# Weight tiles, row fetches and two of four weight sums of a Strassen-type product: DVE additions replaced by adding transfers from GpSimd

## The chip, the core and the metric

One of the eight cores of a Trainium2 chip runs the whole layer as one program. The metric is the device time of one execution in microseconds (us), as the median of several runs. Engines are called as in the profile: PE is TensorE's matrix multiply, PEld its weight load, DVE is VectorE, ACT is ScalarE, POOL is GpSimd and SP is SyncE. SP and POOL mostly issue transfers here: each has a queue that is worked through in order, and an issue that waits holds up everything behind it on that queue.

## The reference, cut to what matters

```python
h = rms_norm(x, norm_in_g[layer])
proj = jnp.einsum('bsd,de->bse', h, w_in[layer])              # 512 x 2048 times 2048 x 19456
(qa, ka, va, za, qb, kb, vb, zb, qm, zm, gates) = jnp.split(proj, split_points, axis=-1)
...                                                            # three attention branches, each * silu(gate path)
g_a, g_b, g_m = jnp.split(jax.nn.sigmoid(gates), N_BRANCH, axis=-1)
merged = (g_a * (ya @ w_proj_a) + g_b * (yb @ w_proj_b) + g_m * (ym @ w_proj_m))
x = x + jnp.einsum('bsd,de->bse', merged, w_out[layer])
return rms_norm(x, norm_final_g)
```

Everything is float32. 512 tokens, width 2048. Most of the work is the product of the normed input with `w_in`; the last is the product of `merged` with `w_out`.

## The kernel before

A float32 operand is split into a rounded part (`whi`, by ACT) and the remainder (`wlo`, by DVE: the tile less the rounded part), and a product is three matmuls: high times high, high times low, low times high. A weight tile is 128 partitions by 1024 columns, 0.5 MB.

**Pairs.** 65 pairs of 128-column units of `w_in` are computed by the class `Pair`: a block product with seven multiplications in place of eight (Winograd's form). The four weight quarters of a pair are called a11 and a12 (first unit, lower and upper half of the depth), a21 and a22 (second unit). Four sums of quarters are needed beside the quarters themselves: s = a21 + a22 (line 436), s + a11 (line 441), a21 + a11 (line 448) and the first s + a11 form plus a12 (line 454: s, already holding a21 + a22 + a11, plus a12). All four are DVE additions on 128x1024 tiles in SBUF. The kernel's signs and forms are arranged so that only additions are needed.

A pair runs in seven steps of 24 matmuls. The weights of the steps are, in order: p1 = a11, p5 = a21 + a22, p6 = that + a11, p2 = a12, q7 = a21 + a11, q3 = p6's tile + a12, p4 = a22. The function `parts_1024` splits each one: ACT writes `whi` (line 387), DVE writes `wlo` (line 388). There are three `whi` and three `wlo` buffers, so the split for a step starts when PE has finished the step three before. Step 3's result x is copied to SBUF by ACT (`hb`, line 456) after the third multiplication (p6), because the fifth (q7) adds on into the same PSUM bank; line 467 reads that bank again after the fifth, before the seventh (p4) adds into it.

**Where the weights come from.** SP issues the four quarter loads of a pair when the pair begins, which is in the last step of the pair before (`self.follower.begin()`). The tiles come from the pool `raw` with 18 buffers. From the forms' preparation on, 12 of these hold the input's forms T1, T2 and T3 until the last pair, so six are left for weight tiles, and a load waits until the buffer's last reader is done.

**Stages.** Memory keys and values; memory-attention queries; a branch with 8 heads (16 pairs); a dilated branch (20 pairs); then the gates: 8 rounds i of 3 pairs each. After each gate pair, DVE multiplies both results with projected rows that POOL fetched from DRAM (`pj`) and adds them up. After the third pair of round i, `merged_forms(i)` makes the forms of the merged rows i and 8+i (lines 920 to 923) and POOL stores them to DRAM (`waiting`, `waiting3`).

**The last product.** `multiply` runs the same seven-step scheme on `w_out`, twice (28 pieces each), with the sums of `w_out` quarters made by DVE. The forms stored in `waiting` are fetched back one row at a time by POOL (`fetch_then`, line 936, into slots of 512 columns or half tiles of 256), a few jobs ahead (`ahead_by`), and split by ACT and DVE into the tiles that held the input's forms (`left`, `right`, `third_form`). Which piece a job stands beside is given by the dictionary `beside`. POOL also fetches rows of x (`res`) and stores and fetches finished rows (`rows_done`).

The Tile framework writes each engine's instructions in one fixed order at build time, by its own estimates, and adds semaphore waits. At run time each engine keeps to that order.

Of the kernel before, what the change touches and what calls it, by code (L numbers as in the profile page):

```python
# [41 lines left out]
def trunk_layer(ctx: ExitStack, tc: tile.TileContext, x, xT, mem, memT, gains, gfin, w_in, w_mem, w_pa, w_pb,  # L42
# [16 lines left out]
    def wide_tile(name, dt=F32):  # L59

        return sb.tile([P, 1024], dt, name=name, tag="raw", bufs=RAWS)
# [314 lines left out]
    def quarter(u, half):  # L376
        raw = wide_tile("raw")
        nc.sync.dma_start(raw, w_in[u][:, half * 1024:(half + 1) * 1024])
        return raw

    def half_tile(name):
        return sb.tile([P, 256], F32, name=name, tag="halft", bufs=4)
# [25 lines left out]
    class Pair:  # L408
# [22 lines left out]
        def steps(self):  # L431
            u1, u2 = self.units
            a11, a21, a22, a12 = quarter(u1, 0), quarter(u2, 0), quarter(u2, 1), quarter(u1, 1)
            s = wide_tile("raw")
            p1 = parts_1024(a11)
            nc.vector.tensor_tensor(s, a21, a22, op=OP.add)  # L436
            yield 0
            p5 = parts_1024(s)
            x = acc_bank()[:, :256]
# [7 lines left out]
            seven(y, p5, "T1", start=True)  # L447
            nc.vector.tensor_tensor(a21, a21, a11, op=OP.add)
            d = half_tile("hd")
# [3 lines left out]
            seven(x, p6, "T2")  # L453
            nc.vector.tensor_tensor(s, s, a12, op=OP.add)  # L454
            b = half_tile("hb")
# [7 lines left out]
            yield 4  # L463
            q3 = parts_1024(s)
            seven(x, q7, "T3")
            g2 = self.g2 = slot("g2")
# [446 lines left out]
    waiting = dram.tile([NK, P, 512], F32, name="waiting")  # L913
    waiting3 = dram.tile([8, P, 256], F32, name="waiting3")

    def merged_forms(k):
        g0, g1 = merged[k], merged[8 + k]
        b11, b12, b21, b22 = g0[:, :256], g0[:, 256:], g1[:, :256], g1[:, 256:]
        u, v = slot("u"), half_tile("v")
        nc.vector.tensor_tensor(u[:, :256], b11, b12, op=OP.subtract)  # L920
        nc.vector.tensor_tensor(v, b22, b12, op=OP.subtract)
        nc.vector.scalar_tensor_tensor(u[:, 256:], u[:, :256], -1.0, b22, op0=OP.mult, op1=OP.subtract)
        nc.vector.scalar_tensor_tensor(b12, u[:, 256:], -1.0, b21, op0=OP.mult, op1=OP.subtract)
        for at, t in ((waiting[k], g0), (waiting[8 + k], g1), (waiting3[k], v)):
            nc.gpsimd.dma_start(at, t)
        two = split(u)
        M["T1"][k] = [p[:, :256] for p in two]
        M["T2"][k] = [p[:, 256:] for p in two]

    def fetch_then(src, shape, use):  # L930

        got = []

        def fetch():
            t = slot("mg") if shape == 512 else half_tile("mg")
            nc.gpsimd.dma_start(t, src)
            got.append(t)

        return fetch, lambda: use(got[0])

    def ahead_by(n, jobs):

        fetches, uses = zip(*jobs)

        def piece(i):
            def run():
                for f in fetches[0 if i == 0 else i + n:i + n + 1]:
                    f()
                uses[i]()
            return run  # L950

        return [piece(i) for i in range(len(jobs))]

    def left(k, form):
        c = slice(0, 256) if form == "B11" else slice(256, 512)
        return fetch_then(waiting[k][:, c], 256, lambda t: split(t, M[form][k]))

    def right(k):
        return fetch_then(waiting[8 + k], 512, lambda t: split(t, kept[8 + k]))

    def third_form(k):
        def use(t):
            if k % 2 == 0:
                M["store"] = wide_tile("T3", F32R)
            h = M["store"][:, k % 2 * 512:(k % 2 + 1) * 512]
            M["T3"][k] = split(t, (h[:, :256], h[:, 256:]))
        return fetch_then(waiting3[k], 256, use)

# [121 lines left out]
    for i in range(8):  # L1090
        pair = (i, 8 + i)
        for n, b in enumerate((0, 1, 2)):
            prs = [fetched(projected[b * NK + dt], "pj") for dt in pair]
            done = gates[i][n]
            if i == 7 and n == 2:
                done.run(2)
                later.extend(ahead_by(2, [left(k, "B11") for k in range(7)]))
                done.run(4)
                prepare(0)
# [12 lines left out]
    beside = {}  # L1112
    for at, job in zip([4 + k for k in range(8)] + [12 + k // 2 for k in range(8)] + [16 + k for k in range(8)],
                       ahead_by(3, [right(k) for k in range(8)] + [third_form(k) for k in range(8)]
                                + [left(k, "T4") for k in range(8)])):
        beside.setdefault(at, []).append(job)
    for cp in range(2):
# [17 lines left out]
        if cp:  # L1135
# [4 lines left out]
            for t in (2, 3, 0, 1):  # L1140
                for c in range(2):
                    rs[t, c] = fetched(rows_done[t, c], "res")
            for at, c in ((46, 0), (47, 1), (48, 3)):
                beside[at] = [lambda c=c: [gained(t, c) for t in (2, 3)]]
            for at, c in ((49, 0), (50, 1), (51, 2)):
                beside[at] = [lambda c=c: [gained(t, c) for t in (0, 1)]]
        multiply(zs, n + 12, "B21", True, True)
# [98 lines left out]
```

## Time and profile before

| What | Value |
|---|---|
| Median of 3 runs | 2002.5 us (2000.59 to 2006.08) |
| The profiled execution | 2006.96 us, its span 2005.2 us |
| PE busy | 1962.0 us, 98% of the span |
| DVE busy | 1530.9 us, 76% |
| ACT busy | 1020.6 us, 51% |
| Mean granted TensorE clock | 0.995 |
| Moved by DMA | 284.82 MB, mean 142 GB/s |

The span starts with the first instruction. Busy time of PE says that a matmul was in the pipeline. The granted clock is 1.00 for 2.4 GHz and falls towards 0.5 for stretches at 1.2 GHz.

### The profile page before, as it was taken

The numbers are of one execution on the slowest core, as the hardware profiler recorded it, in microseconds if no ns is written. First come the engines' busy times: TensorE is split into PE (matmuls) and PEld (weight loads), VectorE is DVE, ScalarE is ACT, GpSimd is POOL, SyncE is SP. The second block draws the span as 40 slices with busy tenths as digits, with TensorE's granted clock in tenths as the row PEclk, the third lists the DMA queues.
The fourth block names the chain that finished last, engine by engine and source line by source line (L and its number), as shares of the span: only waits on it lengthen the run. The fifth ranks groups of instructions, "written<-read, shape, count | busy, mean of one in ns | idle before, by whom it ended". The sixth has DMA issues, their size and how long they took to land.

```text
span 2005.2 us, 34840 instructions
## 1 busy us (share of the span) xinstructions
PE 1962.0 (98%) x14225; PEld 1848.9 (92%) x14225; DVE 1530.9 (76%) x1954; ACT 1020.6 (51%) x1573; POOL 135.3 (7%) x257
## 2 busy tenths in 40 slices
PE   8999999999999999999999999999999999998898
PEld 6889999789999999889999999989999999997676
DVE  5976777259989898258888889747888788777877
ACT  7654565245556665235445464644544444444535
POOL 0000010100000000010000000012000000012210
PEclk9999999999999999999999999999999999999999
DMA  9564434432332334423332322255344443347744
GB/s 365 187 224 154 131 127 148 136 106 98 98 107 94 101 106 153 142 95 96 111 99 91 113 88 98 90 176 188 112 143 148 150 140 128 128 143 275 267 179 147
DMA packets 90017, 284.82 MB, mean 142 GB/s; under 512 B 16672, under 2 KB 17696, under 8 KB 89856
## 3 DMA queue, kind: packets, MB, share of 16 engines
q1 hardware_dynamic: 71904, 225.02, 33.5%
q0 software_dynamic: 17808, 57.56, 8.4%
q8 instruction: 111, 1.82, 0.4%
q14 instruction: 50, 0.41, 0.1%
q10 hardware_dynamic: 144, 0.02, 0.0%
HBM read 251.05 MB, written 31.49 MB: 141 GB/s over the span
## 4 chain that ended last, share of the span: by engine, by line
PE 81%; DVE 6%; DMA 6%; issue 4%; ACT 1%; POOL 1%; ACTq 0%; DVEq 0%; SPq 0%; POOLq 0%
PE acc L397 18%; PE acc L398 18%; PE acc L399 18%; PE acc L112 5%; PE acc L110 5%; PE acc L111 5%; DMA raw<-in_w_in 2%; DVE wlo L388 2%; DMA mg<-waiting 2%; DMA rows_done<-res 1%; PE acc L1043 1%; PE acc L1044 1%; PE acc L1042 1%; ACT whi L387 1%; PE att L162 1%
## 5 line engine op out<-in xcount | busy, mean ns | idle before, releaser
L387 ACT ACTIVATE whi<-raw 128x1024 fp32r<-128x1024 f32 x507 | 537.2, 1060 | 604.0 <-PE acc L398 366.8
L388 DVE TENSOR_TENSOR wlo<-raw,whi 128x1024 fp32r<-128x1024 f32 x507 | 618.0, 1220 | 175.5 <-ACT whi L387 164.7
L397 PE MATMUL acc<-kept,whi 128*128 128x256 f32 x2080 | 588.6, 283 | 11.7 <-DVE g L467 10.9
L398 PE MATMUL acc<-kept,whi 128*128 128x256 f32 x2080 | 585.2, 281 | 0.0
L399 PE MATMUL acc<-kept,wlo 128*128 128x256 f32 x2080 | 584.9, 281 | 0.0
L397 PE MATMUL acc<-T,whi 128*128 128x256 f32 x1560 | 441.7, 283 | 0.5 <-ACT ha L443 0.5
L398 PE MATMUL acc<-T,whi 128*128 128x256 f32 x1560 | 441.0, 283 | 0.0
L399 PE MATMUL acc<-T,wlo 128*128 128x256 f32 x1560 | 441.0, 283 | 0.0
L397 PEld LDWEIGHTS acc<-kept,whi 128*128 128x128 f32 x2080 | 392.8, 189 | 13.7 <-issue 12.8
L398 PEld LDWEIGHTS acc<-kept,whi 128*128 128x128 f32 x2080 | 393.2, 189 | 0.4
L399 PEld LDWEIGHTS acc<-kept,wlo 128*128 128x128 f32 x2080 | 393.2, 189 | 0.0
L397 PEld LDWEIGHTS acc<-T,whi 128*128 128x128 f32 x1560 | 297.9, 191 | 1.0 <-ACT ha L443 0.7
L398 PEld LDWEIGHTS acc<-T,whi 128*128 128x128 f32 x1560 | 298.3, 191 | 0.3
L399 PEld LDWEIGHTS acc<-T,wlo 128*128 128x128 f32 x1560 | 298.2, 191 | 0.0
L91 DVE TENSOR_TENSOR wlo<-raw,whi 128x1024 fp32r<-128x1024 f32 x78 | 94.9, 1223 | 140.7 <-ACT whi L90 140.7
L90 ACT ACTIVATE whi<-raw 128x1024 fp32r<-128x1024 f32 x78 | 82.2, 1059 | 158.9 <-PE acc L111 100.8
L110 PE MATMUL acc<-shi,whi 128*128 128x512 f32 x320 | 126.6, 396 | 0.5 <-ACT pr L145 0.5
L111 PE MATMUL acc<-slo,whi 128*128 128x512 f32 x320 | 126.5, 395 | 0.0
L112 PE MATMUL acc<-shi,wlo 128*128 128x512 f32 x320 | 126.4, 395 | 0.0
L436 DVE TENSOR_TENSOR raw<-raw 128x1024 f32<-128x1024 f32 x65 | 79.5, 1223 | 25.9 <-DMA raw<-in_w_in 24.2
L441 DVE TENSOR_TENSOR raw<-raw 128x1024 f32<-128x1024 f32 x65 | 79.3, 1220 | 0.9
L454 DVE TENSOR_TENSOR raw<-raw 128x1024 f32<-128x1024 f32 x65 | 79.3, 1220 | 0.9
(269 smaller groups left out, 2609.7 us busy)
## 6 DMA issues: line engine op xcount, KB each, us to landing
raw<-in_w_in SPq DMA_DIRECT2D x266, 512.0 KB, 3.7
raw<-in_w_out SPq DMA_DIRECT2D x48, 512.0 KB, 6.5
raw<-in_w_mem SPq DMA_DIRECT2D x32, 512.0 KB, 5.1
projected<-pr POOLq DMA_DIRECT2D x48, 256.0 KB, 2.5
pj<-projected POOLq DMA_DIRECT2D x48, 256.0 KB, 5.4
raw<-in_w_pm SPq DMA_DIRECT2D x16, 512.0 KB, 3.8
raw<-in_w_pa SPq DMA_DIRECT2D x16, 512.0 KB, 4.1
xraw<-in_xT SPq DMA_DIRECT2D x16, 256.0 KB, 6.9
```

The lines of the kernel that those rows point to most:

```text
L90: nc.scalar.activation(hi, raw, AF.Copy)
L91: nc.vector.tensor_tensor(lo, raw, hi.bitcast(F32), op=OP.subtract)
L110: nc.tensor.matmul(ps, whi, hi[i], start=i == 0, stop=False)
L111: nc.tensor.matmul(ps, whi, lo[i], start=False, stop=False)
L112: nc.tensor.matmul(ps, wlo, hi[i], start=False, stop=i == n - 1)
L387: nc.scalar.activation(hi, raw, AF.Copy)
L388: nc.vector.tensor_tensor(lo, raw, hi.bitcast(F32), op=OP.subtract)
L397: nc.tensor.matmul(ps, hi[:, sl], f[0], start=start and k == 0, stop=False, skip_group_check=True)
L398: nc.tensor.matmul(ps, hi[:, sl], f[1], start=False, stop=False, skip_group_check=True)
L399: nc.tensor.matmul(ps, lo[:, sl], f[0], start=False, stop=stop and k == 7, skip_group_check=True)
L436: nc.vector.tensor_tensor(s, a21, a22, op=OP.add)
L441: nc.vector.tensor_tensor(s, s, a11, op=OP.add)
```

## The change

Two of the four weight sums are taken off DVE. Instead of `a21 += a11` and `s += a12` as DVE additions of two SBUF tiles, POOL issues transfers that read the quarter a11 (or a12) from DRAM a second time and add it to the tile in SBUF (`add_quarter`, with `accum_op`). The sum a21 + a22 is now written over a22's tile (s is that tile), so that the separate tile for s is gone, and a22 is loaded a second time, near the end of the pair, for p4. The load of a12 is issued after a pair's first sum.

The fetches of the merged forms go from POOL to SP. Several rows come with one transfer: four or three half rows, two whole rows, or four rows of `v`, which now lie side by side in `waiting3`. They land in wide tiles of the pool `raw`, at pieces that are set by hand (`at`). The split of `v` is done four rows at a time.

```diff
+    def add_quarter(t, u, half):
+        nc.gpsimd.dma_start(t, w_in[u][:, half * 1024:(half + 1) * 1024], accum_op=OP.add)
...
             u1, u2 = self.units
-            a11, a21, a22, a12 = quarter(u1, 0), quarter(u2, 0), quarter(u2, 1), quarter(u1, 1)
-            s = wide_tile("raw")
+            a11, a21, s = quarter(u1, 0), quarter(u2, 0), quarter(u2, 1)
             p1 = parts_1024(a11)
-            nc.vector.tensor_tensor(s, a21, a22, op=OP.add)
+            nc.vector.tensor_tensor(s, a21, s, op=OP.add)
             yield 0
+            a12 = quarter(u1, 1)
             p5 = parts_1024(s)
...
-            nc.vector.tensor_tensor(a21, a21, a11, op=OP.add)
+            add_quarter(a21, u1, 0)
...
-            nc.vector.tensor_tensor(s, s, a12, op=OP.add)
+            add_quarter(s, u1, 1)
...
             q3 = parts_1024(s)
+            a22 = quarter(u2, 1)
...
-    waiting3 = dram.tile([8, P, 256], F32, name="waiting3")
+    waiting3 = dram.tile([2, P, 1024], F32, name="waiting3")
...
+    def fetch(src, shape):
+        t = wide_tile("mg").rearrange("p (k c) -> p k c", c=shape)
+        t = t[:, :src.shape[0]]
+        nc.sync.dma_start(t, src.rearrange("k p c -> p k c"))
+        return t
...
+    def fetch_third(h):
+        fetched_rows["T3", h] = wide_tile("mg")
+        nc.sync.dma_start(fetched_rows["T3", h], waiting3[h])
...
+    def third_form(h):
+        parts = split(fetched_rows.pop(("T3", h)), (wide_tile("T3", F32R), wide_tile("T3", F32R)))
+        for i in range(4):
+            M["T3"][4 * h + i] = [p[:, i * 256:(i + 1) * 256] for p in parts]
...
                 done.run(2)
-                later.extend(ahead_by(2, [left(k, "B11") for k in range(7)]))
-                done.run(4)
+                fetch_left("B11", 0, 4)
+                done.run(1)
+                fetch_left("B11", 4, 3)
+                later.extend([lambda k=k: left("B11", k) for k in range(7)])
+                done.run(3)
                 prepare(0)
...
-    for at, job in zip([4 + k for k in range(8)] + [12 + k // 2 for k in range(8)] + [16 + k for k in range(8)],
-                       ahead_by(3, [right(k) for k in range(8)] + [third_form(k) for k in range(8)]
-                                + [left(k, "T4") for k in range(8)])):
-        beside.setdefault(at, []).append(job)
+    for k in range(8):
+        if k % 2 == 0:
+            at(k, fetch_right, k)
+        at(4 + k, right, k)
+        if k % 4 == 0:
+            at(9 + k // 4 * 2, fetch_third, k // 4)
+            at(13 + k // 4 * 2, third_form, k // 4)
+            at(15 + k, fetch_left, "T4", k, 4)
+        at(19 + k // 4 * 3 + k % 4, left, "T4", k)
```

How this moves instructions is seen in the written order. On DVE, one gate pair before, from the remainder of p6 on (tiles 16351, 16353, 16355, 16357 and 16359 are a11, a21, a22, a12 and s of this pair; 16585 to 16593 those of the next):

```order
L388 TENSOR_TENSOR wlo_16431<-raw_16359,whi_16430 128x1024
L1104 TENSOR_TENSOR g2_16086<-g2_16086,g2_16318 128x512
L388 TENSOR_TENSOR wlo_16463<-raw_16357,whi_16462 128x1024
L454 TENSOR_TENSOR raw_16359<-raw_16359,raw_16357 128x1024
L388 TENSOR_TENSOR wlo_16494<-raw_16353,whi_16493 128x1024
L388 TENSOR_TENSOR wlo_16525<-raw_16359,whi_16524 128x1024
L436 TENSOR_TENSOR raw_16593<-raw_16587,raw_16589 128x1024
L462 TENSOR_TENSOR g1_16522<-acc_16497,ha_16428 128x256
L448 TENSOR_TENSOR raw_16587<-raw_16587,raw_16585 128x1024
```

And the same stretch of a gate pair now (17118, 17120, 17160 and 17292 are a21, s, a12 and the second load of a22; 17353 and 17355 are a21 and s of the next pair):

```order
L391 TENSOR_TENSOR wlo_17195<-raw_17120,whi_17194 128x1024
L1106 TENSOR_TENSOR g2_16850<-g2_16850,g2_17083 128x512
L391 TENSOR_TENSOR wlo_17227<-raw_17160,whi_17226 128x1024
L391 TENSOR_TENSOR wlo_17258<-raw_17118,whi_17257 128x1024
L438 TENSOR_TENSOR raw_17355<-raw_17353,raw_17355 128x1024
L391 TENSOR_TENSOR wlo_17289<-raw_17120,whi_17288 128x1024
L465 TENSOR_TENSOR g1_17286<-acc_17261,ha_17192 128x256
```

The two additions of lines 454 and 448 are gone, and the next pair's first sum (line 438) now stands ahead of the remainder of q3 (`wlo_17289`), where it stood behind it.

On POOL, at the end of a round of the gates, before:

```order
L925 DMA waiting<-g_16086 128x512
L925 DMA waiting_14936<-v 128x256
L491 DMA pj<-projected 128x512
L925 DMA waiting<-g_16056 128x512
L491 DMA pj<-projected 128x512 x5
```

And now, over one round (rows `raw<-in_w_in` are the adding transfers, six in a round):

```order
L929 DMA waiting<-g_15418 128x512
L382 DMA raw<-in_w_in 128x1024
L929 DMA waiting_14979<-v 128x256
L495 DMA pj<-projected 128x512
L929 DMA waiting<-g_15386 128x512
L495 DMA pj<-projected 128x512
L382 DMA raw<-in_w_in 128x1024
L495 DMA pj<-projected 128x512 x2
L382 DMA raw<-in_w_in 128x1024 x2
L495 DMA pj<-projected 128x512 x2
L382 DMA raw<-in_w_in 128x1024 x2
```

The first adding transfer shown is the one into s of a round's first pair; a store of the round before stands ahead of it. The pairs of rows `x2` are the one into s of one pair and the one into a21 of the next.

On SP, the last loads of the gates and the first of the last product, before and now in one piece of the difference:

```order
-L378 DMA raw<-in_w_in 128x1024 x88
-L972 DMA raw<-in_w_out 128x1024 x38
-L1138 DMA gf<-in_gfin 128x1024 x2
-L972 DMA raw<-in_w_out 128x1024 x10
-L1082 DMA out_dram<-res 128x512 x16
-L1242 UNCONDITIONAL_BRANCH
+L971 DMA raw<-in_w_out 128x1024 x3
+L937 DMA mg<-waiting 128x2x512
+L971 DMA raw<-in_w_out 128x1024 x3
+L937 DMA mg<-waiting 128x2x512
+L971 DMA raw<-in_w_out 128x1024 x4
+L937 DMA mg<-waiting 128x2x512
```

The fetches of the merged forms (`mg`) now stand between the loads of `w_out`, where POOL's queue had them.

## Rows read from the trace of the kernel before

**Rows 1.** The page's first part: busy us, share, instructions.
```profile
PE 1962.0 (98%) x14225; PEld 1848.9 (92%) x14225; DVE 1530.9 (76%) x1954; ACT 1020.6 (51%) x1573; POOL 135.3 (7%) x257
```
**Rows 2.** Who waited for whom: us in total, times, longest.
```profile
PE acc L397 <- DVE g L467: 10.9, 8, 3.0
PE acc L1043 <- DVE wlo L388: 9.4, 7, 4.1
...
PE acc L1042 <- ACT whi L387: 4.0, 3, 3.0
```
**Rows 3.** Busy by stretch: bounds, engines (instructions), PEclk, DMA share, GB/s.
```profile
500.00:550.00 50.00, 50.00 (x416) 49.74 (x415) 45.21 (x62) 30.44 (x50) 0.54 (x1) 1.00 0.33 105
...
1550.00:1600.00 50.00, 47.88 (x403) 47.71 (x402) 40.71 (x47) 23.17 (x32) 4.88 (x9) 1.00 0.44 148
...
1850.00:1900.00 50.00, 44.88 (x182) 34.10 (x181) 43.82 (x57) 24.09 (x38) 13.07 (x24) 0.97 0.73 249
```
**Rows 4.** Timeline of PE: start, us, instruction, [idle before it, and releaser].
```profile
1774.09 0.36 PE L397 MATMUL acc<-kept,whi 128*128 128x256 f32 x1 [2.99 <-DVE g L467]
...
1826.44 0.58 PE L1043 MATMUL acc<-wlo,kept 128*128 128x512 f32 x1 [4.07 <-DVE wlo L388]
...
1881.03 0.98 PE L1042 MATMUL acc<-whi,T 128*128 128x512 f32 x2 [3.03 <-ACT whi L387]
...
1927.65 0.50 PE L1043 MATMUL acc<-wlo,shi 128*128 128x512 f32 x1 [2.34 <-DVE wlo L388]
```
**Rows 5.** Busy by stretch, behind the idle time at 1774.
```profile
1774.00:1778.00 4.00, 3.91 (x24) 3.94 (x25) 4.00 (x5) 1.98 (x3) 0.00 (x0) 0.69 0.32 111
```
**Rows 6.** Timeline of DVE in a round's first pair.
```profile
1584.43 1.23 DVE L436 TENSOR_TENSOR raw<-raw 128x1024 f32<-128x1024 f32 x1 [4.07 <-DMA raw<-in_w_in]
```
**Rows 7.** Waits of ACT for fetched rows: us in total, times, longest.
```profile
ACT kept L170 <- DMA mg<-waiting: 20.5, 13, 3.7
```
**Rows 8.** Groups of DVE: count, busy us, mean ns, idle before.
```profile
L454 DVE TENSOR_TENSOR raw<-raw 128x1024 f32<-128x1024 f32 x65 | 79.3, 1220 | 0.9
```
**Rows 9.** Timeline of DVE, remainders: a head's second pair, round's first, round's second.
```profile
546.69 1.22 DVE L388 TENSOR_TENSOR wlo<-raw,whi 128x1024 fp32r<-128x1024 f32 x1
...
1572.74 1.22 DVE L388 TENSOR_TENSOR wlo<-raw,whi 128x1024 fp32r<-128x1024 f32 x1
...
1594.18 1.23 DVE L388 TENSOR_TENSOR wlo<-raw,whi 128x1024 fp32r<-128x1024 f32 x1 [0.59 <-ACT whi L387]
...
1596.58 1.22 DVE L388 TENSOR_TENSOR wlo<-raw,whi 128x1024 fp32r<-128x1024 f32 x1
```
**Rows 10.** Timeline of ACT in the same three pairs.
```profile
553.76 1.06 ACT L387 ACTIVATE whi<-raw 128x1024 fp32r<-128x1024 f32 x1 [1.55 <-issue]
...
1578.04 1.06 ACT L387 ACTIVATE whi<-raw 128x1024 fp32r<-128x1024 f32 x1 [1.54 <-PE acc L398]
...
1600.37 1.06 ACT L387 ACTIVATE whi<-raw 128x1024 fp32r<-128x1024 f32 x1 [1.55 <-issue]
1601.33 0.35 ACT L456 COPY hb<-acc 128x256 f32<-128x256 f32 x1
1603.16 1.06 ACT L387 ACTIVATE whi<-raw 128x1024 fp32r<-128x1024 f32 x1 [1.47 <-PE acc L398]
```
**Rows 11.** Timeline of POOL in the round's first pair.
```profile
1573.95 0.55 POOL L925 DMA_DIRECT2D waiting<-g  x1 [56.39 <-ACT ha L443]
```
**Rows 12.** Transfers: issuer, count, KB each, median us from issue to landing.
```profile
raw<-in_w_in SPq DMA_DIRECT2D x266, 512.0 KB, 3.7
...
pj<-projected POOLq DMA_DIRECT2D x48, 256.0 KB, 5.4
...
yf<-ydram POOLq DMA_DIRECT2D x14, 256.0 KB, 3.2
```
**Rows 13.** Loads of w_in, from issue to landing.
```profile
DMA to landing us min/median/max: 3.1/3.7/9.0
```
**Rows 14.** Queues: packets, MB, share of 16 engines' span.
```profile
q1 hardware_dynamic: 71904, 225.02, 33.5%
```

More of the change, by code (lines that the diff above doesn't have):

```diff
@@ L923, in merged_forms @@
         nc.vector.scalar_tensor_tensor(b12, u[:, 256:], -1.0, b21, op0=OP.mult, op1=OP.subtract)
-        for at, t in ((waiting[k], g0), (waiting[8 + k], g1), (waiting3[k], v)):
+        for at, t in ((waiting[k], g0), (waiting[8 + k], g1), (waiting3[k // 4][:, k % 4 * 256:(k % 4 + 1) * 256], v)):
             nc.gpsimd.dma_start(at, t)
@@ L928, in merged_forms, with fetch_left, fetch_right, left @@
         M["T2"][k] = [p[:, 256:] for p in two]
[L930 to L954, printed above, removed]
-        c = slice(0, 256) if form == "B11" else slice(256, 512)
-        return fetch_then(waiting[k][:, c], 256, lambda t: split(t, M[form][k]))
-    def right(k):
[L959 to L967, printed above, removed]
+    def fetch(src, shape):
[3 more added lines that the diff above has]
+        return t
+    fetched_rows = {}
+    def fetch_left(form, k, n):
+        c = slice(0, 256) if form == "B11" else slice(256, 512)
+        t = fetch(waiting[k:k + n, :, c], 256)
+        for i in range(n):
+            fetched_rows[form, k + i] = t[:, i]
+    def fetch_right(k):
+        t = fetch(waiting[8 + k:10 + k], 512)
+        for i in range(2):
+            fetched_rows["B2", k + i] = t[:, i]
+    def fetch_third(h):
+        fetched_rows["T3", h] = wide_tile("mg")
+        nc.sync.dma_start(fetched_rows["T3", h], waiting3[h])
+    def left(form, k):
+        split(fetched_rows.pop((form, k)), M[form][k])
+    def right(k):
+        split(fetched_rows.pop(("B2", k)), kept[8 + k])
+    def third_form(h):
+        parts = split(fetched_rows.pop(("T3", h)), (wide_tile("T3", F32R), wide_tile("T3", F32R)))
+        for i in range(4):
+            M["T3"][4 * h + i] = [p[:, i * 256:(i + 1) * 256] for p in parts]
     def piece(c, i):
@@ L1112, in trunk_layer, with at @@
     beside = {}
-    for at, job in zip([4 + k for k in range(8)] + [12 + k // 2 for k in range(8)] + [16 + k for k in range(8)],
-                       ahead_by(3, [right(k) for k in range(8)] + [third_form(k) for k in range(8)]
-                                + [left(k, "T4") for k in range(8)])):
-        beside.setdefault(at, []).append(job)
+    def at(n, f, *args):
+        beside.setdefault(n, []).append(lambda: f(*args))
+    for k in range(8):
[7 more added lines that the diff above has]
+        at(19 + k // 4 * 3 + k % 4, left, "T4", k)
     for cp in range(2):
@@ L1142, in trunk_layer @@
                     rs[t, c] = fetched(rows_done[t, c], "res")
[L1143 to L1146, printed above, removed]
+            for job, c in ((46, 0), (47, 1), (48, 3)):
+                for t in (2, 3):
+                    at(job, gained, t, c)
+            for job, c in ((49, 0), (50, 1), (51, 2)):
+                for t in (0, 1):
+                    at(job, gained, t, c)
         multiply(zs, n + 12, "B21", True, True)
```

## The prediction

> **What bounds the kernel now.** I read the page's busy shares first, then who PE waits for, then the timeline around each of those waits, then the pair's own steps on DVE and ACT. PE is busy 98% of the span and DVE 76% [rows 1]. Where DVE is busiest in the attention stages, PE has no idle time at all: 45.2 of 50 us on DVE beside 50.00 on PE [rows 3]. So DVE work as such is not in the way. The reader should look for the few places where PE does stop. They are three groups of waits: 10.9 us in the gates, where the seventh step waits for line 467, and 9.4 + 4.0 us in the last product, where a step waits for the parts of its weight tile [rows 2]. That is 24.3 us, and nothing more can be won by shortening what PE waits for. A long wait costs a little extra: in the 4 us behind the 2.99 us idle at 1774 the granted clock is 0.69, part of them at 1.2 instead of 2.4 GHz, so about 0.31 x 4 = 1.2 us more [rows 4, 5]. I count 1.2 for each of the four waits over 2.3 us.
>
> The cause of the gates' waits is a weight load. In a round's first pair DVE sits idle 4.07 us for the next pair's first sum (line 436), because its tile has not landed [rows 6], and line 467 stands behind that in DVE's order. The load was late since its buffer was: with six buffers and five tiles per pair, all taken when the pair begins, a load waits for sums that the end of a round delays. In the last product, ACT waits 20.5 us in 13 pieces for rows that POOL fetches one at a time [rows 7], and the splits of the weights stand behind these waits.
>
> **Removed.** 65 x 2 DVE additions of 1.22 us, 159 us of DVE [rows 8]. Alone they are worth 0: DVE idles 0.9 us before line 454 in 65 pairs together, and PE is full where DVE is fullest [rows 3]. The wide tile for s goes, and a11 is free after its use in line 441 and not only after line 448. Each load of a pair is then released by a split or sum about a whole pair ahead of its use, and the last to be released, that of a22, by the remainder of p2. In the pair of 1594 that remainder ends at 1596.58 + 1.22 = 1597.8 [rows 9]; 3.7 us later [rows 12], at 1601.5, the tile is there, the next first sum ends at 1602.7, and the remainder of q3, which now stands behind it, at 1603.9. PE's step 4 starts when ACT gets a buffer, at about 1603.1 [rows 10], its step 5 some 2.8 us later at 1605.9. So there is 2 us of slack, and the wait for line 467 has no cause any more: 10.9 + 1.2 = 12.1 us gained.
>
> **Fetches.** The waits of ACT for fetched rows should vanish, as SP brings two to four rows at once and some pieces ahead. PE's idle there is 9.4 + 4.0 = 13.4 us [rows 2]. Of it the 2.34 at 1927 [rows 4] comes long after these fetches and stays; two long waits bring 2 x 1.2 of clock; that leaves 13.5 us. But DVE is 88% busy in that stretch [rows 3], the same splits and the same `w_out` sums remain, the fetches now take wide tiles from the weights, and in SP's queue a fetch that waits for a store holds up the `w_out` loads behind it. The gain lies between 13.5 and a loss of the same size; I take half, 6.7 us.
>
> **Added: the adding transfers.** The one into a21 may start when the first sum has read it (1602.7 above) and is needed by the split for q7 of the next pair, 14 us later: cost 0. The one into s is close. It may start when the remainder of p6 is done. It must have landed before ACT splits q3; and behind that split on ACT stands the copy `hb`, which must be done before PE's step 4. In the pair of 1594: p6's remainder ends at 1595.4 [rows 9]; the split of q3 stood at 1600.37, `hb` ended at 1601.7, step 4 started at 1603.1 [rows 10], so the split may come 1.4 us later, at 1601.8. The room is 6.4 us. In a round's first pair it is 1572.74 + 1.22 = 1573.96 to 1578.04 + 1.4, 5.5 us, and a store of 0.55 us stands ahead on POOL [rows 9 to 11]. In the second pair of a head it is 547.9 to 555.2, 7.3 us [rows 9, 10]. Going through all pairs this way, 13 have about 5.5 us (7 of them a round's first, with the store ahead), 15 about 6.4, 19 about 7.2 and 18 more. Behind a waiting adding transfer POOL holds the next pair's one into a21, the `pj` fetches of that pair and the stores; all of them are wanted a pair or more later, so this queue costs nothing by itself.
>
> No adding transfer is in this trace. The nearest row is the load of the same 0.5 MB, 3.7 us from issue to landing [rows 12]. The tile in SBUF must also be read once: 8 rows of 4 KB per DMA engine; a packet took 0.335 x 16 x 2005.2 / 71904 = 0.15 us at 3.1 KB [rows 14], 0.19 at 4 KB, so 1.5 us. With 0.3 for busier engines I take 5.5 us. The ends are 3.2 us, a POOL fetch of half the size [rows 12], if the add costs nothing, and 9.0, the slowest load of w_in [rows 13]. A gain below zero cost is excluded: nothing waited for the additions (0.9 us idle before line 454 in 65 [rows 8]). At 5.5 the seven first pairs lose 0.65 each, six others 0.1, the rest 0: 5 us.
>
> The Trainium skill, Collectives: The Full Stack (The bandwidth ceiling: the fold count and why AG ≠ RS ≠ AR), says that an add inside a transfer is not slow for its arithmetic but for its two source reads, which share one read ring and halve the rate. By it the second pass of 1.5 us is right; with one pass only, 4.0 us, all pairs would hide it and the 5 us fall away. No run here shows it yet.
>
> **Sum.** 12.1 + 6.7 - 5 = 13.8 us off the profiled execution's 2006.96, which is 1993.2. That execution lies 4.5 above the median of 2002.5, so I predict 2002.5 - 13.8 = 1988.7, rounded to 1989.
>
> **Rivals.**
> *The sum into s lands late* (slower). Place: step 4 of a pair, PE waiting for `hb`, which stands behind q3's split on ACT. For it: with three more tiles per pair (4 loads become 5, and 2 adds), the gates' DMA rate goes from 148 GB/s to about 148 + 3 x 1.57 MB / 59 us (three pairs of 7 x 2.8 us) = 228, and the share from 0.44 to 0.68, or 0.8 with the second pass [rows 3]; a POOL fetch of 256 KB took 3.2 us where it stood alone and 5.4 where five came in a row [rows 12]. If the adding transfer grows by the same 2.2 to 7.7, the loss is 7 x 2.85 + 6 x 2.3 + 15 x 1.4 + 19 x 0.5 = 64 us, and 13 x 1.2 of clock: 2002.5 - 18.8 + 80 = 2064. It decides from the point where it takes back 18.8 us: 7 x (L - 4.85) + 6 x (L - 5.4) + 15 x (L - 6.3) gives L = 6.4 us, 0.9 above my value. Against it: the loads of a pair are released one by one, so at most one runs beside it.
> The Trainium skill, DMA: Bandwidth & Descriptors (Issuing engines are not separate DMA queues), speaks for this rival: transfers of all issuers share the same 16 DMA engines and interleave. The 3.2 and 5.4 us agree.
>
> *The loads are late instead* (slower). The next first sum stands ahead of q3's remainder, so a load of a22 that takes over 5.7 us stops PE at step 5. At 6.7 us the 24 gate pairs lose 1 us each: 2002.5 - 13.8 + 24 = 2013. For it the 9.0 us maximum, against it the median [rows 13].
>
> *Nothing moves.* The waits of rows 2 are on DVE's results, and the end of a round gives DVE the same extra work as before; if half of the 12.1 stays, the last product gives nothing and the 5 us are paid, the time is 2001.5.
>
> **Chances.** Forecast 0.50, sum into s late 0.28, loads late 0.10, nothing moves 0.12. A difference under 0.3% (6 us) can hardly be told from no change. Faster by more: 0.52 (the forecast, and a mild form of the loads' rival). Same: 0.15 (nothing moves, and the first rival close to 6.4 us). Slower: 0.33. The low end, 1977, is close to all of 24.3 + 4 x 1.2 = 29 us gained, 1973; the high end, 2045, takes in the first rival up to about 7.3 us. For the forecast alone 1979 to 1996.
>
> **What the profile would show.** Right: no PE wait on line 467's successor at the rounds' ends; DVE near 1370 us; ACT's wait for `mg` near 0; adding transfers with 5 to 6 us to landing; no PE wait on `hb` beyond 1 us. Wrong: a wait of PE for ACT's `hb` copy, or of ACT's split for a DMA into `raw`, repeated in every pair, with the clock below 1.00 in the gates (first rival); DVE idle before the first sum with a DMA as releaser (second); waits as in rows 2 (third). The landing of the adding transfers, 6.4 us or not, decides most of it.

## The result: 2031 us, slower by 1.35%

The changed kernel takes 2031.2 us (median of 4 runs, 2029.7 to 2034.0) beside 2003.9 us for the kernel before on the same chip. The ratio is 1.0135, 95% interval 1.0116 to 1.0155. The profiled execution spans 2030.0 us, 24.8 more than before. The forecast was 1989.

The page after, first its busy shares, then the transfers (count, KB each, median us from issue to landing):

```profile
PE 1973.4 (97%) x14225; PEld 1856.6 (91%) x14225; DVE 1385.4 (68%) x1818; ACT 1016.6 (50%) x1567; POOL 232.1 (11%) x356
```
```profile
raw<-in_w_in SPq DMA_DIRECT2D x331, 512.0 KB, 5.3
raw<-in_w_in POOLq DMA_DIRECT2D x130, 512.0 KB, 6.0
...
pj<-projected POOLq DMA_DIRECT2D x48, 256.0 KB, 8.5
```

DVE lost 145 us of work against [rows 1], and the time did not fall. PE's matmuls are as many as before, but PE is busy 11.4 us longer; the other 13.4 us are idle time of PE. The lower clock is about half of the 11.4: its mean is 0.992 where it was 0.995, and the share that was not granted, summed over the time in which PE is busy, is 13.0 us where it was 6.7. The rest is not taken apart. The 130 adding transfers landed in 6.0 us, and the plain loads beside them in 5.3 instead of 3.7 [rows 12]. Taken by kind, the 65 adding transfers into s landed in 5.4 us in the median (5.2 to 9.4), the 65 into a21 in 6.4.

Where the time went is read from PE's timeline: the start of the first matmul of pair 0, of the first pair of each stage, and of the last product. A stage is the time between two such starts. Differences to the kernel before, in us, each from one profiled execution, here with the experiments told below:

| Kernel | memory attention (pairs 0 to 6) | 8 heads (7 to 22) | dilated (23 to 40) | gates (41 to 64) | last product |
|---|---|---|---|---|---|
| after | +16.2 | 0.0 | +4.7 | +10.8 | -6.4 |
| both sums on DVE | +0.7 | +0.4 | -0.9 | -3.7 | -10.1 |
| only a21 added by transfer | +0.4 | +0.4 | +0.4 | -12.6 | -9.1 |
| only s added by transfer | +14.6 | 0.0 | +11.4 | +15.6 | -8.0 |
| after, first sum later | +5.9 | +0.1 | +7.6 | -0.6 | -10.8 |
| only a21, first sum later | +5.5 | +0.1 | -0.3 | -12.3 | -9.1 |

(Pairs 5 and 6 are the first head's; pairs 21 and 22, the dilated branch's first two, run with the last head; in the first gate pairs the dilated branch's attention ends.) Most of the loss is in the first column, of which the prediction did not speak.

Who PE waits for now: us in total, times, longest.

```profile
PE acc L400 <- ACT hb L459: 8.7, 12, 2.7
PE att L161 <- ACT shi L170: 6.2, 2, 3.9
...
PE att L628 <- ACT p L617: 5.4, 4, 2.0
PE acc L1042 <- DVE wlo L391: 5.4, 5, 2.1
PE acc L402 <- DVE wlo L391: 5.3, 6, 2.0
PE acc L1041 <- ACT whi L390: 3.5, 2, 3.1
```

The first row of [rows 2], PE waiting for `g` of line 467, is gone. In its place PE waits for `hb`, and in the memory attention for ACT's splits and probabilities. Two engines now stand still for transfers, as the waits of ACT and of DVE show:

```profile
ACT whi L390 <- DMA raw<-in_w_in: 117.8, 40, 5.8
ACT kept L170 <- DMA mg<-waiting: 11.8, 5, 5.5
ACT shi L170 <- DMA mvr<-mvd: 7.7, 2, 4.6
```
```profile
DVE raw L438 <- DMA raw<-in_w_in: 161.5, 57, 6.1
```

ACT waits at line 390 in 40 of the 65 pairs: that is q3's split, for the adding transfer into s (the view of line 382 names the same 117.8 us in 40 waits as what others waited for it, and gives a landing of 5.2 to 9.5 us). DVE waits at line 438, the next pair's first sum, for a plain load, in 57 pairs. Before, ACT's splits of the pairs waited for no transfer, and DVE's group of first sums (busy us, mean ns, idle time before it and what ended most of it) was:

```profile
L436 DVE TENSOR_TENSOR raw<-raw 128x1024 f32<-128x1024 f32 x65 | 79.5, 1223 | 25.9 <-DMA raw<-in_w_in 24.2
```

How one pair stalls: the first pair of a round, 1661.3 us is its first matmul. POOL, ACT, DVE and PE (start, us, instruction, idle time before it and what ended it):

```profile
1666.22 0.85 POOL L382 DMA_DIRECT2D raw<-in_w_in  x1 [0.55 <-DVE wlo L391]
1666.76 0.88 POOL L929 DMA_DIRECT2D waiting<-v  x1
1667.33 0.87 POOL L495 DMA_DIRECT2D pj<-projected  x1
```
```profile
1674.23 1.06 ACT L390 ACTIVATE whi<-raw 128x1024 fp32r<-128x1024 f32 x1 [5.76 <-DMA raw<-in_w_in]
1675.19 0.35 ACT L459 COPY hb<-acc 128x256 f32<-128x256 f32 x1
```
```profile
1676.91 1.23 DVE L438 TENSOR_TENSOR raw<-raw 128x1024 f32<-128x1024 f32 x1 [7.11 <-issue]
1678.06 1.22 DVE L391 TENSOR_TENSOR wlo<-raw,whi 128x1024 fp32r<-128x1024 f32 x1
```
```profile
1675.60 0.38 PE L400 MATMUL acc<-T,whi 128*128 128x256 f32 x1 [2.72 <-ACT hb L459]
```

The transfer into s is issued at 1666.2 and lands 7.9 us later, just before ACT's split starts, with stores and `pj` fetches sent right behind it. ACT stands still 5.76 us, `hb` behind it is late, and PE waits 2.72. DVE has meanwhile stood 7.1 us at the next first sum. The profile names no releaser here, but a load that was issued at 1667.8 took 9.1 us, so that it landed just before the sum starts. So q3's remainder, behind it, ends at 1679.3, 18.0 us after the pair's first matmul; where nothing stalls it is wanted at 14.3. This pair took 24.5 us; one that nothing stalls takes 20.0.

In the memory attention the same two waits meet the softmax. A stretch of the chain of waits there (start, us, what):

```profile
244.24 5.32 DMA raw<-in_w_in
...
249.65 0.15 DVE raw L438
...
250.79 0.16 DVE l L615
250.95 0.59 DVE nm L608
251.54 1.13 DVE wlo L391
...
252.76 0.27 SPq L378
...
253.12 0.42 SPq L623
...
253.59 6.99 DMA mvr<-mvd
...
260.67 0.38 ACT shi L170
```

A load takes 5.3 us, DVE's first sum waits for it, and behind that sum in DVE's order stand the softmax's small sums (lines 608 and 615) and a remainder; that remainder frees the buffer of the next load, behind which SP holds the fetch of the attention's values (`mvr`), 7.0 us more; ACT waits for these, and PE for ACT. The clock follows: a mean of 0.94 from 250 to 300 us, a part of it at the lower level of 1.2 GHz, with PE busy 40.27 of 50 us. Before, the same stretch had 49.91 and 1.00. The two rows, before and after (columns as in [rows 3]):

```profile
250.00:300.00 50.00, 49.91 (x395) 48.38 (x394) 37.75 (x52) 30.12 (x56) 5.48 (x10) 1.00 0.39 132
```
```profile
250.00:300.00 50.00, 40.27 (x285) 37.31 (x284) 27.63 (x40) 24.46 (x46) 7.09 (x11) 0.94 0.57 169
```

### The profile page after: what moved, and what is told of

The parts are those of the page before. It is cut to its first block, busy times and chain, and to the rows that moved or that the text cites. A ratio compares the mean times of both kernels' runs of the same rounds, so it can differ in the third digit from the quotient of the medians.

```text
span 2030.0 us, 35154 instructions
## 1 busy us (share of the span) xinstructions
PE 1973.4 (97%) x14225; PEld 1856.6 (91%) x14225; DVE 1385.4 (68%) x1818; ACT 1016.6 (50%) x1567; POOL 232.1 (11%) x356
## 4 chain that ended last, share of the span: by engine, by line
PE 67%; issue 13%; DMA 10%; DVE 5%; ACT 2%; POOL 1%; SPq 0%; ACTq 0%; POOLq 0%; DVEq 0%
PE acc L400 15%; PE acc L401 14%; PE acc L402 14%; DMA raw<-in_w_in 8%; PE acc L112 3%; PE acc L110 3%; PE acc L111 3%; DVE wlo L391 2%; PE acc L1042 2%; PE acc L1043 2%; PE acc L1041 2%; ACT whi L390 1%; DMA mg<-waiting 1%; DMA raw<-in_w_out 1%; PE att L162 1%
## 5 line engine op out<-in xcount | busy, mean ns | idle before, releaser
L400 PEld LDWEIGHTS acc<-T,whi 128*128 128x128 f32 x1560 | 298.7, 191 | 15.4 <-ACT hb L459 12.6
L382 POOL DMA_DIRECT2D raw<-in_w_in x130 | 113.6, 874 | 1054.1 <-DVE raw L438 433.2
L438 DVE TENSOR_TENSOR raw<-raw 128x1024 f32<-128x1024 f32 x65 | 79.6, 1225 | 177.4 <-DMA raw<-in_w_in 161.5
L444 DVE TENSOR_TENSOR raw<-raw 128x1024 f32<-128x1024 f32 x65 | 79.3, 1220 | 0.9
```

The costliest lines, as they stand in the source:

```text
L382: nc.gpsimd.dma_start(t, w_in[u][:, half * 1024:(half + 1) * 1024], accum_op=OP.add)
L400: nc.tensor.matmul(ps, hi[:, sl], f[0], start=start and k == 0, stop=False, skip_group_check=True)
L438: nc.vector.tensor_tensor(s, a21, s, op=OP.add)
```

## Experiments

The experiments ran in four rounds. The kernel before took 2004.7 to 2006.7 us in them, so times of different rounds compare to within 2 or 3 us. The ratios are each to the kernel before of the same round.

**Both sums back on DVE.** The new tiles and fetches stay.

```diff
-            add_quarter(a21, u1, 0)
+            nc.vector.tensor_tensor(a21, a21, a11, op=OP.add)
...
-            add_quarter(s, u1, 1)
+            nc.vector.tensor_tensor(s, s, a12, op=OP.add)
```

> Undoes one part: the two sums that became adding transfers are made on VectorE again; the new order of the weight fetches (five 512 KB loads a pair, the sum of a21 and a22 made in a22's tile) and the new fetches of the last product stay. Theory A (the adding transfers' traffic is the loss: 130 more transfers of 512 KB, the median load 5.3 us instead of 3.7): the loads land near 4 us again, the first project product of the memory-attention stage starts near 364 us as before (not 379), the gates' wait for the sum of g comes back in part; 1990 to 2003 us. Theory B (the order of the fetches is the loss: a load is issued only when a later tile is free, and the first sum waits for it on VectorE): the 15 us of the memory-attention stage stay, the mark is at 375 to 380 us, 2018 to 2032 us.

Measured: 1993.6 us, 0.9931 (0.9917 to 0.9946), as theory A had it. Median load 3.8 us, memory attention +0.7. So the order of the fetches is not the loss by itself; with the adding transfers on top of it 38 us are lost. In the gates the wait that the prediction saw ended by the new order is still there under its new line number, smaller:

```profile
PE acc L400 <- DVE g L471: 8.6, 8, 1.9
```

**Only the adding transfers, on the kernel before.**

```diff
-            nc.vector.tensor_tensor(a21, a21, a11, op=OP.add)
+            add_quarter(a21, u1, 0)
...
-            nc.vector.tensor_tensor(s, s, a12, op=OP.add)
+            add_quarter(s, u1, 1)
```

> One part alone: the kernel before, with only the two sums a21+a11 and s+a12 of a pair made by adding transfers; four loads a pair and their order stay. Theory A (the transfers' traffic, six of 512 KB a pair in place of four): the loss is mostly there, median load 4.7 us or more, the mark near 375 us, 2012 to 2028 us. Theory B (the order of the fetches): the adding transfers do no harm by themselves, 1988 to 2003 us, the mark near 364 us.

Measured: 2014.4 us, 1.0045 (1.0027 to 1.0063). The time is in theory A's range, but against the kernel before that is only 9 us, while the same two transfers cost 38 on the new order. The memory attention, where theory A put the loss, takes 3.3 us more. ACT waits for the transfers as long as in the changed kernel, but DVE's wait at the first sum is 5.2 us, where it was 161.5:

```profile
ACT whi L390 <- DMA raw<-in_w_in: 119.3, 42, 5.2
```
```profile
DVE raw L439 <- DMA raw<-in_w_in: 5.2, 9, 1.7
```

So each theory held half of it: the transfers and the order cost most together.

**VectorE's sums in the first seven pairs.**

```diff
-            add_quarter(s, u1, 1)
+            if u1 in by_dve:
+                nc.vector.tensor_tensor(s, s, a12, op=OP.add)
+            else:
+                add_quarter(s, u1, 1)
```
(and the same for a21; `by_dve` holds the first units of these seven pairs)

> The changed kernel with VectorE's sums in place of the adding transfers in the first seven pairs only (memory attention and the first values), adding transfers in the other 58. Theory A: the 15.7 us that are lost up to the first project product (364 to 379 us) go, 2013 to 2018 us. Theory B (the order of the fetches): they stay, 2028 to 2033 us.

Measured: 2015.1 us, 1.0051 (1.0030 to 1.0072), in theory A's range; single executions go from 2010.1 to 2026.2, and the profiled one is the fastest. In it the memory attention is back to +1.1 us, the gates stay at +6.2. By the medians 16 us belong to seven of 65 pairs.

**Only the last product's new fetches, on the kernel before.** The pairs' edits of the change are left out, its `fetch`, `fetch_left`, `fetch_right`, `fetch_third` and the pieces set by `at` are kept.

> One part alone: the kernel before with only the last product's rows fetched in wide tiles by SyncE and split four at a time; pairs as before. In the changed kernel the last product took as long as before (both 24.8 us late at its first product and at its end), so both theories expect 1996 to 2006 us. A third theory, that its wide tiles give 6 us there which late weight loads ate, expects 1992 to 1997 us.

Measured: 2000.9 us, 0.9970 (0.9956 to 0.9984). The last product is 6.8 us shorter, and no other stage moves by more than 1.1. Both theories had the time, but not the reason: I had read the last product of the changed kernel as equal, from two marks inside it; from its first matmul to the end it gained 6.4 us there as well.

**One transfer at a time.**

```diff
-            add_quarter(s, u1, 1)
+            nc.vector.tensor_tensor(s, s, a12, op=OP.add)
```

> The changed kernel with only a21+a11 by an adding transfer; s+a12 is VectorE's sum again (six 512 KB transfers a pair). The kernel with both sums on VectorE took 1993.6 us, the changed one 2031.2. Theory T (traffic: each of the two adding transfers lengthens every landing, and costs half): 2006 to 2018 us, median load about 4.5 us, PE's waits for hb small. Theory W (waits: only the transfer into s is waited for, its split stands ahead of the copy hb on ScalarE, as the prediction's first rival had it): 1990 to 1998 us, since the transfer into a21 is wanted a step later than it lands.

```diff
-            add_quarter(a21, u1, 0)
+            nc.vector.tensor_tensor(a21, a21, a11, op=OP.add)
```

> The changed kernel with only s+a12 by an adding transfer; a21+a11 is VectorE's sum again. Theory T (traffic): half the cost again, 2006 to 2018 us, the same as with only a21+a11 within 5 us. Theory W (waits for the transfer into s): nearly all the cost, 2020 to 2031 us, with 6 us or more of PE's waits for hb between 1300 and 1850 us.

Measured: only a21 1987.0 us, 0.9905 (0.9891 to 0.9920), the fastest of all; only s 2040.2 us, 1.0167 (1.0142 to 1.0192). T fell: it had the cost in equal halves. All of the cost is in the transfer into s, as W had it, though both times lie outside W's ranges, by 3 and by 9 us. The a21 transfer lands later than the other, in 7.1 us (5.4 for the one into s in its kernel), and the loads beside it take 4.6, yet nobody waits: its split comes more than half a pair after it may start. With it PE's wait for `g` is nearly gone:

```profile
PE acc L400 <- DVE g L471: 1.6, 4, 0.8
```

With only s, ACT's and DVE's waits are those of the changed kernel:

```profile
ACT whi L390 <- DMA raw<-in_w_in: 124.4, 43, 5.3
```
```profile
DVE raw L438 <- DMA raw<-in_w_in: 177.8, 58, 6.1
```

The 6 us of waits for `hb` that W wanted were 5.3 in 9 waits; more came through q3's remainder (8.0) and the softmax (9.8).

**The bytes without the wait.** Plain stores to DRAM of the summed tiles, which nobody reads: on the kernel with both sums on DVE, as shown, and the second one alone on the kernel with only a21 by transfer.

```diff
             nc.vector.tensor_tensor(a21, a21, a11, op=OP.add)
+            store_aside(a21)
...
             nc.vector.tensor_tensor(s, s, a12, op=OP.add)
+            store_aside(s)
```

> Both sums on VectorE (1993.6 us without more), and behind each a plain store by GpSimd of the summed tile (512 KB) to DRAM that nobody reads: the bytes on the transfer engines are those of the changed kernel, and a tile is held until its store has read it, but no split waits for a transfer in the place of a sum. Theory T (traffic): the median load goes from 3.8 to 4.8 us or more and the time to 2012 to 2031 us. Theory W (waits): 1993 to 2003 us.

> The kernel with only a21+a11 by an adding transfer (1987 us), and behind VectorE's sum s+a12 a plain store by GpSimd of s to DRAM that nobody reads: as many bytes on the transfer engines as in the changed kernel, but no split waits for them. Theory D (deadline of the transfer into s): 1987 to 2000 us. Theory T (bytes): 2015 to 2031 us.

Measured: two stores 2006.1 us, 1.0004 (0.9993 to 1.0016), 12 more than without and between the two theories' ranges; the a21 transfer and one store of s 1991.6 us, 0.9933 (0.9915 to 0.9951), as theory D had it, 4.6 more than without the store, with intervals that overlap. So bytes cost something, up to 12 us, 6.6 of them in the gates. But the transfer into s costs 44 us (2031.2 less 1987.0), and a store of the same tile in its place a tenth of that. A store differs from an adding transfer in direction and lands sooner (3.8 us), so this is a guide to the bytes' part and does not measure it exactly. The kernel with one store shows one thing more: DVE's wait at the first sum rose to 125.6 us, from 86.7 without the store, and that cost next to nothing. This wait alone is not the loss either.

```profile
DVE raw L445 <- DMA raw<-in_w_in: 125.6, 52, 5.6
```

**`hb` by DVE.**

```diff
-            nc.scalar.copy(b, x)
+            nc.vector.tensor_copy(b, x)
```

> The changed kernel with the copy hb of bank x made by VectorE in place of ScalarE, where it stands behind the next pair's first sum and ahead of q3's remainder: it no longer waits for the transfer into s. Theory W (the gates' loss is PE's wait for hb behind q3's split): PE's 8.7 us of waits for hb go to below 2 us and the time falls by 6 to 10 us, to 2021 to 2025 us. Theory T (late landings of all kinds): hb then stands behind the first sum, which waits for a load, and the wait moves there; 2028 to 2036 us.

Measured: 2067.3 us, 1.0312 (1.0284 to 1.0341): both theories missed the time, W by the sign; T had the place. On DVE the copy stands behind the next pair's first sum, and that wait is worse than ACT's:

```profile
PE acc L400 <- DVE hb L459: 34.0, 21, 3.2
```

This is what pointed to the first sum as a second place where a whole engine stands.

**Half a transfer into s.**

```diff
-            add_quarter(s, u1, 1)
+            nc.vector.tensor_tensor(s[:, 512:], s[:, 512:], a12[:, 512:], op=OP.add)
+            add_quarter(s[:, :512], u1, 1)
```
(`add_quarter` then reads as many columns as its tile has)

> The changed kernel with the adding transfer into s cut to half a tile (256 KB, the left half; VectorE adds the right half, about 0.65 us). Known so far: without this transfer 1987 us, with the whole of it 2031. Theory D (a deadline: what counts is when q3's split can start, and in an undisturbed pair it starts 8.7 us after the pair's first matmul, some 5 us after the transfer is asked for): a half lands 1 us or more earlier and most of the 44 us go, 1988 to 2005 us, ScalarE's waits for the transfer below 40 us in place of 118. Theory T (the bytes): half of the cost stays, 2006 to 2015 us.

Measured: 2011.5 us, 1.0030 (1.0018 to 1.0042). Halves land in 3.7 us, and ACT's waits fall to 19.4 us, as D wanted; but only 20 of 44 us come back, which is the time that theory T gave. They come back in the gates (-5.0 instead of +10.8) and the dilated branch (+0.6). The memory attention stays at +18.9, where DVE still waits at the first sum and ACT for `mvr` (10.9 us). Theory D alone is not enough; nor can bytes be half of the cost, since a store of the whole tile cost 4.6 us.

**The first sum later.** It gets a factor of one that is made from q3's remainder, so DVE can no longer stand at it ahead of that remainder.

```diff
+            if self.after:
+                nc.vector.scalar_tensor_tensor(s, a21, self.after.one, s, op0=OP.mult, op1=OP.add)
...
             q3 = parts_1024(s)
+            self.one = sb.tile([P, 1], F32, name="one", bufs=2)
+            nc.vector.tensor_scalar(self.one, q3[1][:, :1].bitcast(F32), 0.0, 1.0, op0=OP.mult, op1=OP.add)
```

> The changed kernel, its two adding transfers kept, with the first sum of a pair (a21+a22) forced behind the remainder of the previous pair's q3 on VectorE, by a factor of one that is made from that remainder (a 128x1 operation more a pair). Theory Q (the loss needs both queues: VectorE stands at the first sum for the load of a22, 161 us in all, with q3's remainder and the softmax's small sums behind it, while ScalarE stands at q3's split for the transfer into s): VectorE's wait at the first sum falls below 60 us and the time to 2005 to 2020 us. Rival (ScalarE's wait alone): 2028 to 2036 us, or more because p5 is split later.

Measured: 2011.7 us, 1.0025 (1.0009 to 1.0042), inside theory Q's range and 16 below the rival's. The group of the sum, and ACT's wait beside it:

```profile
L439 DVE SCALAR_TENSOR_TENSOR raw<-raw,one 128x1024 f32<-128x1024 f32 x61 | 78.4, 1285 | 3.5 <-DMA raw<-in_w_in 0.9 <-DVE one L472 0.3 <-DVE m L866 0.3
```
```profile
ACT whi L390 <- DMA raw<-in_w_in: 126.1, 45, 5.4
```

ACT waits as long as ever for the transfer, and yet 20 us are back: +5.9 in the memory attention, -0.6 in the gates. So nearly half of the loss was where DVE stood in its order.

**Both cures, and the later sum where no split waits.** The edit of the later sum is put on the kernel with half a transfer into s, and on the one with only a21.

> Both cures together: the adding transfer into s cut to half a tile (2011.5 us alone), and the first sum forced behind the remainder of the previous pair's q3 (2011.7 us alone). Theory Q2 (two queue heads: ScalarE at q3's split for the transfer into s, VectorE at the first sum for a load; each cure takes one of them): the gains add up, 1986 to 1996 us, and the first project product starts within 4 us of the kernel before. Rival (each cure gave the same 20 us, and the rest, 24 us, is the transfers' bytes or GpSimd's queue): 2005 to 2013 us.

> The fastest version so far (only a21+a11 by an adding transfer, 1987 us) with the first sum forced behind the previous pair's q3 remainder. Theory Q2: VectorE's 87 us at the first sum had room there, since no split waits for a transfer; the time stays within 4 us, 1983 to 1991 us. Rival (VectorE's wait at the first sum costs by itself): 1972 to 1982 us.

Measured: half of s with the later sum 2003.5 us, 0.9983 (0.9969 to 0.9997); only a21 with the later sum 1992.3 us, 0.9927 (0.9912 to 0.9942). The first is a miss for both theories: the gains do not add up. The second lies 1 us above theory Q2's range and far from its rival's. Part of the reason is in it: the later sum itself costs 4 to 5 us, all in the memory attention (+5.5 against +0.4). There the transfer into a21 has to wait for the first sum, and POOL holds the attention's fetches behind it: in that kernel ACT waits 5.9 us for `mkr` and DVE 8.0 for `z`, against 0.8 for each with the early sum. What is left between the two is 11 us by the medians; in the profiled executions, which are 16 apart, 10 are in the gates and 5 in the dilated branch, though ACT's waits are down to 27.7 us. That remainder is open. The second kernel also prices ACT's wait by itself: with the later sum, the transfer into s costs 19 us (2011.7 less 1992.3), with the early one 44. On the old order it is about 14, an estimate: 2014.4, less 7 for the fetches, less the 1993.9 of the next run.

**The a21 transfer with the old order of fetches.** The kernel before with the last product's new fetches and:

```diff
-            nc.vector.tensor_tensor(a21, a21, a11, op=OP.add)
+            add_quarter(a21, u1, 0)
```

> The kernel before with the last product's new fetches (2000.9 us without more) and a21+a11 by an adding transfer; four loads a pair in the old order. If the transfer into a21 is what ends the stalls at the gates' rounds, whatever the order of the fetches: 1984 to 1991 us, no wait of PE for the sum of g above 1 us. If the gain of the a21 transfer needs the new order: 1996 to 2003 us.

Measured: 1993.9 us, 0.9944 (0.9928 to 0.9960), between the two cases. Both are in it: the gates gain 11.7 us, as with the new order, PE's wait for `g` is 1.2 us; and the memory attention loses 8.9, by POOL's queue. The transfer waits for the first sum, which is late in this order, and `z` and `mkr` stand behind it:

```profile
287.75 0.90 POOL L382 DMA_DIRECT2D raw<-in_w_in  x1 [21.15 <-DVE raw L439]
288.32 1.44 POOL L494 DMA_DIRECT2D z<-zdram  x2
289.38 0.91 POOL L494 DMA_DIRECT2D mkr<-mkd  x1
```

With the new order the same three are issued ten microseconds earlier:

```profile
277.82 0.90 POOL L382 DMA_DIRECT2D raw<-in_w_in  x1 [15.34 <-DVE l L615]
278.39 1.42 POOL L495 DMA_DIRECT2D z<-zdram  x2
279.45 0.89 POOL L495 DMA_DIRECT2D mkr<-mkd  x1
```

## Why the prediction was wrong, step by step

**"PE has no idle time", three groups of waits.** Right as a reading of the kernel before, but it led me to price the change only at the places where PE stood before. The memory attention had hardly any waits of PE (0.8 us) and so no row in the prediction; it lost 16.2 of the 24.8 us.

**"The wait for line 467 has no cause any more: 12.1 us gained."** The size was right by luck, the cause was not. With the new order alone, 8.6 of the 10.9 us stay and the gates gain 3.7 us. With the a21 addition taken off DVE they gain 12.6, or 11.7 with the old order. There DVE still waits 1.9 to 4.0 us for a load at the first sum in seven rounds, and PE's waits for `g` are down to 1.2 us in all. So the sentence that the removed additions alone "are worth 0", since DVE idles 0.9 us before line 454 [rows 8], failed: idle time before an addition says that nothing held it up, not that nothing stood behind it. The end of a round was the load and DVE's own work together, with one addition of 1.22 us too many behind the load. Nor was that load late by its buffer alone. The one that DVE waits for in [rows 6] was issued at 1577.9 and landed 6.4 us later, beside stores and `pj` fetches of POOL; the one at 1597.8, with none beside it, took 3.2. Who waited for the first, and its landing:

```profile
DVE raw L436: 4.1, 1
...
DMA to landing us min/median/max: 6.4/6.4/6.4
```

**"Fetches: half of 13.5, 6.7 us."** Measured -6.8 us alone and -6.4 in the changed kernel. The half was a choice between two bounds, and it came out, in part by luck: in the twelve other kernels with the same fetches this stage gained 7.1 to 11.4 us. ACT's wait for `mg` fell from 30.0 to 11.8 us, not near 0. The prediction counted 20.5 [rows 7] and left out the waits under another tile's name:

```profile
ACT T L170 <- DMA mg<-waiting: 9.5, 4, 5.4
```

**"The one into a21: cost 0."** Right: 1987.0 us with it, 1993.6 without.

**"Cost 5 us" for the one into s.** This step failed; it is 44 us. The landing was not the error: the transfers into s took 5.4 us in the median where the prediction had 5.5, with single ones up to 9.4. Put into the prediction's own formula, 5.4 gives 7 x 0.55 = 4 us; even 6.0, the median of both kinds, gives 7 x 1.15 + 6 x 0.6 = 12. And the landing stayed below the 6.4 us that were to decide most of it. The formula was the error. It gave every pair a room of its own with all else in its place, and held that "at most one" load runs beside the transfer. It did not ask what the transfer does to that load. The load that ends DVE's wait at the next first sum took 3.8 us in the median with both sums on DVE, and as long with only a21; it took 5.5 with only s and 5.4 in the changed kernel. DVE's waits there went from 87.7 us to 177.8 and 161.5. So the prediction's second rival, the first sum that waits for a load ahead of q3's remainder, is set off by the transfer of the first, even where that one lands in time. The trace before had such a load, the 6.4 us above; the rival was priced against the median of all loads, 3.7.

Taken apart, the forced later sum gives back 20 us and half a transfer 20 us, both together 28; of the other 16 the later sum itself costs 4 to 5, and 11 stay open. I had given the two rivals 0.28 and 0.10 as if only one could come; both came, and both of the signs named for them are in the trace, the first in 40 of 65 pairs.

**"This queue costs nothing by itself."** It held in the changed kernel, where nothing waits for `z` or `mkr`. It failed in the two kernels with only a21 by transfer and a late first sum: POOL's fetches of `z` and `mkr` stand behind the transfer, and the memory attention takes 5 to 9 us more.

**The second pass.** Where only s is added by transfer, loads land in 3.9 us and the adding transfers in 5.4, 1.5 more, the figure that the prediction took for reading the tile. That agreement is partly chance: the same difference is 0.7 us in the changed kernel and 2.5 with only a21, and the two kinds are issued by different engines. The Trainium skill, Collectives: The Full Stack (The bandwidth ceiling: the fold count and why AG ≠ RS ≠ AR), says of the add in a ReduceScatter that it needs two source reads, which share one ring. A longer landing does not contradict it, but no run here shows what the extra time is.

**The sum.** Forecast -12.1 - 6.7 + 5 = -13.8. Measured by stage: gates +10.8 (forecast -7.1), last product -6.4 (-6.7), memory attention +16.2, dilated +4.7 (both 0), and half a microsecond ahead of the first pair.

## What to carry to other kernels

When work moves from an engine to a transfer, ask for each engine what is the next instruction that waits for any transfer, and what stands behind it in that engine's order. Two such places in one pair are not independent: here the transfer of the one made the load of the other land later. Price a load by its landing at the place where it is waited for, not by the median of all. Price a change in every stage that runs the changed code, above all those where nothing waits yet and much small work stands behind the same queues. Of several moved sums, move first the one whose result is wanted last: here one of the two, taken alone, took 7 us off the time and the other added 47 (1987.0 and 2040.2 against 1993.6).

## What the runs showed of the hardware

An adding transfer of 0.5 MB took POOL 0.87 us to issue, where a plain store of the same size took 0.55, and 5.2 us at least to land, where a plain load took 3.1 at least. A 0.5 MB load landed in 3.2 us with no transfer of POOL beside it and in 6.4 (before) and 9.1 (changed) at the end of a round, with several.

A stall of PE costs more than its idle time: of the changed kernel's 24.8 us, 13.4 are idle and 6.3 are the same 14225 matmuls at a lower clock (13.0 less 6.7), about half as much again. In the memory attention the clock fell in two places, to a mean of 0.83 from 260 to 270 us and 0.88 from 290 to 300, so for a part of each at 1.2 instead of 2.4 GHz; in the first a wait of 2.30 us ends, in the second one of 3.91. From 250 to 260 and from 280 to 290 us, with waits of at most 1.75, it stayed at 1.00. The prediction had counted 1.2 us for each wait above 2.3.
